# Strassen's products on eight of sixteen blocks of values and gate in six heads, in place of four

## The chip, the cores and the metric

The kernel runs on one core of one Trainium2 chip. The metric is the device time of one execution in microseconds (us). Its engines are TensorE (PE, with its weight loads PEld), VectorE (DVE), ScalarE (ACT), GpSimd (POOL) and SyncE (SP), which here only issues loads. Each engine works through its own instructions in a fixed order and waits where an operand or a buffer is not ready.

## The reference

Two layers on 256 tokens of width 2048, in float32: a retention layer (8 heads, keys of 256, values of 512 per head) and a pooling layer. The change touches the projections of the retention layer alone:

```python
def retention_layer(x, g_norm, w_in, gn, w_out):
    h = rms_norm(x, g_norm)
    p = h @ w_in
    q, k, v, z = jnp.split(p, [...], axis=-1)
    q = rope(q...); k = rope(k...) * (RET_HEAD_QK ** -0.5)
    o = chunkwise_retention(q, k, v)
    ...                                    # group norm of o per head
    o = o.astype(x.dtype) * jax.nn.silu(z)
    return o @ w_out
```

Per head, v and z (the gate) are each `[256, 2048] @ [2048, 512]`.

## The kernel before

**Precision.** Every operand of a float32 product is split into a part `hi` that TensorE takes in its float32r form and a rest `lo`: ScalarE casts `hi` (L98), VectorE subtracts `lo = src - hi` (L99). A product is then three matmuls, hi·hi, hi·lo and lo·hi, added up in one bank of PSUM (`Sum.add`, L195).

**Tiles.** The 2048 inputs of the projection are 16 blocks of 128, the tokens two halves of 128. Weights arrive in units of `[128, 2048]` float32 (1 MB), three of which can be in flight or in use (`raw`, `bufs=3`); their split halves live in five buffers of 1024 columns of hi and of lo (`w`, `bufs=5`).

**A head** takes twelve units: four for queries and keys (QK units: 16 pairs of a 512- and a 256-column matmul each, L129 and L130, into banks 4 to 7, evicted as `hl` and `qk` by L138 and L139), and eight for values and gate, in the order of `HEAD_ORDER`. Between the two lie the rotation of queries and keys on VectorE (`tcos`, `tsin`, `qk`, L338 to L342, then the split into `qs`), the scores (`sc`, ten matmuls, bank 4) and their mask (`sm`, L361 to L363). A unit of kind v or z holds four blocks of values or of gate and costs 24 matmuls of 512 columns. A unit S holds two blocks of each, `strassen_blocks` says which, and `strassen_unit` takes them by Strassen's seven products, 21 matmuls: VectorE first forms sums of weight blocks from the raw unit (`tc`, L221; `ts`, L223 and L224), which are split like weights (`w<-tc`, `w<-ts`); the sums on the side of the activations (`forms`) are made once, in head 0, by `sides` and lie in a part of `os` that the last head fills. The products p1, p5, p6, p7 lie in banks 5, 6, 4 and 7, and c11, c21 (values) and c12, c22 (gate) in banks 0 to 3. After the last S unit L388 to L392 combine the p's; at the end of a head follow `vs`, `po`, the group norm (`ors`), `og`, and eight transposes (`turned`, L453) that are split into `os` (L103, L104) while TensorE is at the next head's QK units.

**Order.** The program is written head by head; a scheduler then lays each engine's instructions in an order of its own, which is fixed when the program is built. VectorE and ScalarE thus prepare units ahead of TensorE, as far as five `w` buffers let them.

Of the kernel before, what the change touches and what calls it, by code (L numbers as in the profile page):

```python
# [13 lines left out]
P = 128  # L14
D = 2048
S = 256
KT = D // P
NH = 8
DV = 512
VT = 2 * D // P  # L20
# [12 lines left out]
SUMS = ("p1", "p5", "p6", "p7", "c11", "c21", "c12", "c22")  # L33


HEAD_ORDER = ("vvvvzzzz",) + ("vvvSzSzz",) * (NH - 1)
HEAD_BANKS = {"c11": 0, "c21": 1, "c12": 2, "c22": 3, "p6": 4, "p1": 5, "p5": 6, "p7": 7}


def strassen_blocks(first, j):  # L40

    k = first + 4 * (j // 2) + j % 2
    return k, k + 2
# [7 lines left out]
def kernel(  # L51
# [56 lines left out]
    def load(src):  # L108
        raw = wpool.tile([P, UNIT], F32, tag="raw", name="raw", bufs=3)
        nc.sync.dma_start(out=raw, in_=src)  # L110
        return raw
# [138 lines left out]
    hs = act.tile([P, KT, 2, S], F32R, tag="hs", name="hs")  # L250


    with tc.tile_pool(name="rt", bufs=1) as rt:
# [10 lines left out]
        for u in range(4):  # L264
# [6 lines left out]
            for i in range(2):  # L271
                w = wpool.tile([P, 2, HALF], F32R, tag="w", name="w", bufs=5)
                hi, lo = w[:, 0], w[:, 1]
# [42 lines left out]
        unit = 4  # L316


        forms = os[:, VT - 4 :].rearrange("p k a s -> p (k a s)").rearrange("p (i f l t) -> p i f l t", f=4, l=2, t=P)

        def tokens(k, t):
            ts = slice(t * P, (t + 1) * P)
            return hs[:, k, 0, ts], hs[:, k, 1, ts]

        for h in range(NH):
# [40 lines left out]


            order = HEAD_ORDER[h]
            strassen, plain = order.count("S"), {"v": 2 * order.count("S"), "z": 2 * order.count("S")}
            sums = {}  # L370
            for name, i in HEAD_BANKS.items():
                n = 3 * strassen * (name != "c22") + 12 * order.count("v") * (name[0] == "c")
                if n:
                    sums[name] = Sum(i, name, n)
            vt = rt.tile([P, 2, DV], F32, tag="vt", name="vt")
            gz = rt.tile([P, 2, DV], F32, tag="gz", name="gz")
            done = 0
            for kind in order:
                unit += 1
                if kind == "S":  # L380
                    s = [rt.tile([P, 2, 512], F32, tag=tag, name=tag[:2]) for tag in ("tcos", "tsin")]
                    k1, k2 = strassen_blocks(0, done)
                    strassen_unit(
                        load(ret_in[unit - 1]), s, (tokens(k1, 0), tokens(k2, 0), tokens(k2, 1)), forms[:, done], sums
                    )
                    done += 1
                    if done == strassen:
                        nc.scalar.copy(vt[:, 0], sums["p1"].tile)  # L388
                        nc.vector.tensor_tensor(out=vt[:, 1], in0=sums["p6"].tile, in1=vt[:, 0], op=ALU.add)
                        nc.vector.tensor_tensor(out=gz[:, 0], in0=sums["p5"].tile, in1=vt[:, 1], op=ALU.subtract)  # L390
                        nc.vector.tensor_tensor(out=vt[:, 1], in0=sums["p7"].tile, in1=vt[:, 1], op=ALU.add)
                        nc.vector.tensor_tensor(out=gz[:, 1], in0=sums["p5"].tile, in1=vt[:, 1], op=ALU.subtract)  # L392
                    continue
                halves = weights(ret_in[unit - 1])
                for i, (hi, lo) in enumerate(halves):
                    for j in range(2):
                        for t in range(2):
                            ws = slice(j * 512, (j + 1) * 512)
                            sums[f"c{t + 1}{1 + 'vz'.index(kind)}"].add(*tokens(plain[kind], t), hi[:, ws], lo[:, ws])
                        plain[kind] += 1  # L400


            vs = rt.tile([P, 2, 2, DV], F32R, tag="vs", name="vs")
# [26 lines left out]
                nc.scalar.activation(sq, po[t], AF.Square, accum_out=var[:, t : t + 1])  # L430
            nc.vector.tensor_scalar(out=var, in0=var, scalar1=1.0 / DV, scalar2=EPS, op0=ALU.mult, op1=ALU.add)
            rsqrt(ors, var)
            if h == 0:
                a = rt.tile([P, 4, S], F32, tag="tcos", name="a")
                x = rt.tile([P, 2, P], F32, tag="tsin", name="x")
                sides(hs, 0, 0, a, x, forms)


            og = rt.tile([P, 2, DV], F32, tag="tcos", name="og")
# [260 lines left out]
def _layout(inputs):  # L700

    import numpy as np

    f = np.float32

    def units(w):
        k, n = w.shape
        w = w.reshape(k // P, P, n // P, P).transpose(2, 1, 0, 3).reshape(n // P, P, k)
        if k == 2 * UNIT:
            w = w.reshape(n // P, P, 2, UNIT).transpose(0, 2, 1, 3)  # L710
        elif 2 * k == UNIT:
            w = w.reshape(n // P // 2, 2, P, k).transpose(0, 2, 1, 3)
        return np.ascontiguousarray(w).reshape(-1, P, UNIT)

    def head_units(v, z, order):
        units, j = [], 0
        plain = {"v": 2 * order.count("S"), "z": 2 * order.count("S")}
        for kind in order:
            if kind == "S":
                k1, k2 = strassen_blocks(0, j)  # L720
                units.append(np.stack([z[k1], v[k1], z[k2], v[k2]]))
                j += 1
            else:
                units.append((v if kind == "v" else z)[plain[kind] : plain[kind] + 4])
                plain[kind] += 4
        return np.stack(units).transpose(0, 2, 1, 3).reshape(-1, P, UNIT)

    def mixed_units(w, first):
        w = w.reshape(VT, P, 4, 512)
        units = []  # L730
        for c in (0, 2):
            classic, j = iter(CLASSIC), 0
            for kind in ORDER:
                if kind == "C":
                    k, i = next(classic)
                    k4 = 4 * classic_blocks(first)[k]
                    units.append(w[k4 : k4 + 4, :, c + i])
                else:
                    k1, k2 = strassen_blocks(first, j)
                    units.append(np.stack([w[k1, :, c + 1], w[k1, :, c], w[k2, :, c + 1], w[k2, :, c]]))  # L740
                    j += 1
        return np.stack(units).transpose(0, 2, 1, 3).reshape(-1, P, UNIT)

    def by_partition(v):
        return v.reshape(-1, P).T

    w = inputs["ret_w_in"][0]
    q = units(w[:, :D]).reshape(NH, 2, P, UNIT)
    k = units(w[:, D : 2 * D]).reshape(NH, 2, P, UNIT)
    v = w[:, 2 * D : 4 * D].reshape(KT, P, NH, DV)  # L750
    z = w[:, 4 * D :].reshape(KT, P, NH, DV)
    vz = np.stack([head_units(v[:, :, h], z[:, :, h], HEAD_ORDER[h]) for h in range(NH)])
    ret_in = np.concatenate([q, k, vz], axis=1).reshape(-1, P, UNIT)
    first = ret_in[:4].reshape(4, P, 4, 4, P).transpose(2, 1, 3, 0, 4).reshape(4, P, UNIT)
    ret_in = np.concatenate([first, ret_in[4:]])
    w = inputs["pool_w_in"][0]
    u = units(w[:, : 2 * D]).reshape(NG, GT, P, UNIT)
    z = units(w[:, 2 * D :]).reshape(NG, GT, P, UNIT)
    pool_in = np.concatenate([u, z], axis=1).reshape(-1, P, UNIT)
    pool_grp = np.concatenate([units(m) for m in inputs["pool_w_grp"][0]])  # L760

    vecs = np.concatenate(
        [
            by_partition(inputs["ret_norm"][0]),
            by_partition(inputs["pool_norm"][0]),
            by_partition(inputs["ret_gn"][0]),
            by_partition(inputs["pool_b_grp"][0]),
            by_partition(inputs["pool_scale"][0]),
        ],
        axis=1,  # L770
    )

    half = np.arange(P, dtype=f)
    inv = f(10000.0) ** (-half / f(P))
    ang = np.arange(S, dtype=f)[None, :] * inv[:, None]
    rope = np.stack([np.cos(ang), np.sin(ang)], axis=1)
    lg = np.log1p(-np.exp2(f(-5.0) - np.arange(NH, dtype=f)))
    diff = (np.arange(S)[None, None, :] - np.arange(S).reshape(2, P, 1)).astype(f)
    m = np.where(diff[None] >= 0, np.exp(np.maximum(diff, f(0.0))[None] * lg[:, None, None, None]), f(0.0))
    masks = (m * f(1.0 / 16.0)).transpose(0, 2, 1, 3).reshape(NH, P, 2 * S)  # L780
    masks = np.concatenate([masks[:, :, :S], masks[:, :, S + P :]], axis=2)
    t = np.arange(S)
    icnt = np.stack([f(1.0) / np.minimum(t + 1, w).astype(f) for w in WINDOWS])
    icnt = np.broadcast_to(icnt[None], (P, NG, S))

    return {
        "xT": inputs["x"][0].T.reshape(KT, P, S).transpose(1, 0, 2),
        "xN": inputs["x"][0].reshape(2, P, D).transpose(1, 0, 2),
        "ret_in": ret_in,
        "ret_out": mixed_units(inputs["ret_w_out"][0], FIRST[0]),  # L790
        "pool_in": pool_in,
        "pool_grp": pool_grp,
        "pool_out": mixed_units(inputs["pool_w_out"][0], FIRST[1]),
        "vecs": vecs,
        "g_last": np.broadcast_to(inputs["final_norm"], (P, D)),
        "rope": rope,
        "masks": masks,
        "icnt": icnt,
        "ident": np.eye(P, dtype=f),
    }  # L800
# [18 lines left out]
```

## Time and profile before

| | |
|---|---|
| median of 3 runs | 1362.15 us (1361.92 to 1362.23) |
| the profiled execution | 1361.73 us |
| its span in the trace | 1359.4 us |
| TensorE busy | 1347.6 us, 99% |
| weight loads / VectorE / ScalarE busy | 84% / 79% / 54% |
| one middle head (239.06 to 307.94 us) | 68.88 us |

The span runs from the first to the last recorded instruction; 2.3 us of the profiled execution lie around it. Busy shares are averages over the span; for this change the stretch of one head matters, which repeats seven times from 101 us on.

### The profile page before, as it was taken

The page shows a single profiled execution, that of the slowest core. Times are in us where ns is not written, and L with a number is a line of the kernel's source. Part 1 is how long each engine was busy: PE and PEld are TensorE (multiplying, and loading weights), DVE is VectorE, ACT ScalarE, POOL GpSimd, SP SyncE. Part 2 cuts the span into 40 slices and gives each one's busy share as a digit, 9 for nine tenths or more (in the row PEclk, how much of TensorE's full clock was granted, in tenths as well). Part 3 has the DMA queues.
Part 4 walks back from the last instruction along what each step waited for, and adds up shares of the span by engine and source line. Part 5 has one row for each costly group of instructions (what it writes and reads, how often), then busy time and mean ns, then how long its engine had stood idle before and what let it go on. Part 6 is the DMA issues. An engine that isn't in the chain of part 4 may idle for free.

```text
span 1359.4 us, 17755 instructions
## 1 busy us (share of the span) xinstructions
PE 1347.6 (99%) x6846; PEld 1145.6 (84%) x6846; DVE 1073.6 (79%) x1550; ACT 731.6 (54%) x1031; POOL 25.5 (2%) x34
## 2 busy tenths in 40 slices
PE   9999999999999999999999999999999999999997
PEld 7888888888888888878888888888888888888886
DVE  7868787878787878798677867876886896888676
ACT  7455555555555555555555545445545545555444
POOL 0000000000000000000000000000000000000102
PEclk9999999999999999999999999999999999999999
DMA  8555546464645455575556555555555555555552
GB/s 338 182 192 174 203 164 213 161 217 161 213 164 200 171 193 177 188 247 201 181 185 213 188 190 187 190 200 190 196 190 186 187 188 192 191 207 212 186 214 95
DMA packets 38196, 262.64 MB, mean 193 GB/s; under 512 B 4368, under 2 KB 4496, under 8 KB 7392
## 3 DMA queue, kind: packets, MB, share of 16 engines
q1 hardware_dynamic: 36432, 255.41, 54.3%
q0 software_dynamic: 1536, 5.57, 1.3%
q8 instruction: 54, 0.88, 0.2%
q10 hardware_dynamic: 144, 0.52, 0.1%
q14 instruction: 30, 0.25, 0.0%
HBM read 259.39 MB, written 2.10 MB: 192 GB/s over the span
## 4 chain that ended last, share of the span: by engine, by line
PE 98%; DVE 1%; ACT 0%; DMA 0%; issue 0%; DVEq 0%; SPq 0%; ACTq 0%
PE c L195 43%; PE acc L129 29%; PE acc L130 15%; PE p L195 6%; PE po L427 1%; PE acc L286 1%; PE acc L287 1%; PE turned L453 1%; PE sc L352 0%; DMA xin<-in_ret_in 0%; PE sc L357 0%; ACT w L98 0%; PE turned L562 0%; DVE w L99 0%; DVE tsin L339 0%; DVE tcos L338 0%
## 5 line engine op out<-in xcount | busy, mean ns | idle before, releaser
L99 DVE TENSOR_TENSOR w<-raw,w 128x1024 fp32r<-128x1024 f32 x472 | 558.1, 1192 | 140.7 <-ACT w L98 136.4
L98 ACT CAST w<-raw 128x1024 fp32r<-128x1024 f32 x472 | 479.1, 1026 | 275.5 <-PE c L195 172.8
L129 PE MATMUL acc<-hs,w 128*128 128x512 f32 x1472 | 516.3, 394 | 0.0
L130 PE MATMUL acc<-hs,w 128*128 128x256 f32 x1472 | 413.4, 281 | 0.0
L129 PEld LDWEIGHTS acc<-hs,w 128*128 128x128 f32 x1472 | 275.7, 187 | 61.8
L195 PE MATMUL c<-w,hs 128*128 128x512 f32 x1284 | 303.9, 390 | 0.0
L195 PEld LDWEIGHTS c<-w,hs 128*128 128x128 f32 x1284 | 239.1, 188 | 49.6
L130 PEld LDWEIGHTS acc<-hs,w 128*128 128x128 f32 x1472 | 278.0, 189 | 1.8
L195 PE MATMUL c<-w,os 128*128 128x512 f32 x666 | 162.6, 392 | 0.0
L195 PE MATMUL c<-w,gs 128*128 128x512 f32 x624 | 147.1, 390 | 0.0
L195 PEld LDWEIGHTS c<-w,os 128*128 128x128 f32 x666 | 124.4, 188 | 26.8 <-ACT w L98 0.3
L195 PEld LDWEIGHTS c<-w,gs 128*128 128x128 f32 x624 | 117.0, 188 | 24.8
L138 ACT COPY hl<-acc 128x256 f32<-128x256 f32 x96 | 35.6, 372 | 147.2 <-PE acc L130 147.2
L129 PE MATMUL acc<-ms,w 128*128 128x512 f32 x256 | 89.0, 390 | 0.0
L130 PE MATMUL acc<-ms,w 128*128 128x256 f32 x256 | 72.2, 282 | 0.0
L98 ACT CAST w<-s 128x1024 fp32r<-128x1024 f32 x32 | 33.5, 1049 | 53.9 <-PE c L195 48.6
L99 DVE TENSOR_TENSOR w<-s,w 128x1024 fp32r<-128x1024 f32 x32 | 39.1, 1223 | 24.6 <-ACT w L98 24.5
L129 PEld LDWEIGHTS acc<-ms,w 128*128 128x128 f32 x256 | 48.0, 188 | 10.1
L130 PEld LDWEIGHTS acc<-ms,w 128*128 128x128 f32 x256 | 48.4, 189 | 0.0
L195 PE MATMUL p<-w,os 128*128 128x512 f32 x150 | 40.9, 390 | 0.0
L195 PE MATMUL p<-w,forms 128*128 128x512 f32 x144 | 39.8, 397 | 0.5 <-ACT forms L98 0.5
L195 PEld LDWEIGHTS p<-w,forms 128*128 128x128 f32 x144 | 27.0, 188 | 7.5 <-ACT forms L98 1.0
(184 smaller groups left out, 1024.7 us busy)
## 6 DMA issues: line engine op xcount, KB each, us to landing
raw<-in_ret_in SPq DMA_DIRECT2D x92, 1024.0 KB, 5.0
raw<-in_pool_in SPq DMA_DIRECT2D x64, 1024.0 KB, 5.0
raw<-in_ret_out SPq DMA_DIRECT2D x32, 1024.0 KB, 5.0
raw<-in_pool_out SPq DMA_DIRECT2D x32, 1024.0 KB, 5.1
raw<-in_pool_grp SPq DMA_DIRECT2D x16, 1024.0 KB, 5.0
xin<-in_ret_in SPq DMA_DIRECT2D x3, 1024.0 KB, 11.4
xn<-in_xN POOLq DMA_DIRECT2D x4, 512.0 KB, 6.8
out<-xn SPq DMA_DIRECT2D x8, 256.0 KB, 2.3
```

What stands on the lines that cost most here:

```text
L98: nc.scalar.copy(hi, src)
L99: nc.vector.tensor_tensor(out=lo, in0=src, in1=hi.bitcast(F32), op=ALU.subtract)
L129: nc.tensor.matmul(acc, hi, moving[:, k], start=(k == 0), stop=False)
L130: nc.tensor.matmul(acc[:, :S], lo, moving[:, k, 0], start=False, stop=(k == n - 1))
L138: nc.scalar.copy(t, acc[:, S:])
L195: nc.tensor.matmul(self.tile, a, w, start=(self.done == 0), stop=(self.done == self.n - 1))
L286: nc.tensor.matmul(accs[c], hi[:, b], hs[:, k], start=(k == 0), stop=False)
L287: nc.tensor.matmul(accs[c][:, :S], lo[:, b], hs[:, k, 0], start=False, stop=(k == KT - 1))
L427: nc.tensor.matmul(po[t], ss[:, p, queries], vs[:, keys, q], start=first, stop=last)
L453: nc.tensor.transpose(turned[:, j * S + t * P : j * S + (t + 1) * P], og[:, t, (2 * i + j) * P : (2 * i + j + 1) * P], idt)
```

## The change

Heads 1 to 6 take four S units in place of two, in the order v S v S S z S z in place of v v v S z S z z. Head 0 (none) and head 7 (two) stay as they were, since the second part of the sums of activations lies where head 6 puts its result. The second pair of sums is made in head 0 by a second call of `sides`. The layout of the weights in memory follows the new order; the bytes stay the same. `head_blocks` gives the order of blocks to kernel and layout alike.

```diff
-HEAD_ORDER = ("vvvvzzzz",) + ("vvvSzSzz",) * (NH - 1)
+HEAD_ORDER = ("vvvvzzzz",) + ("vSvSSzSz",) * (NH - 2) + ("vvvSzSzz",)
+HEAD_FORMS = 4
+def head_blocks(order):
+    products = {k for j in range(order.count("S")) for k in strassen_blocks(0, j)}
+    rest = {c: iter([k for k in range(KT) if k not in products]) for c in "vz"}
+    for kind in order:
+        unit = {"v": "vvvv", "z": "zzzz", "S": ""}[kind]
+        held = [(c, next(rest[c])) for c in unit]
+        yield kind, held
...
-        forms = os[:, VT - 4 :].rearrange(...)
+        forms = [
+            os[:, VT - 4 - 4 * i : VT - 4 * i].rearrange(...)
+            for i in range(HEAD_FORMS // 2)
+        ]
...
-                n = 3 * strassen * (name != "c22") + 12 * order.count("v") * (name[0] == "c")
+                n = 3 * strassen * (name != "c22") + 3 * (KT - 2 * strassen) * (name[0] == "c")
...
-            for kind in order:
+            for kind, held in head_blocks(order):
...
-            if h == 0:
+            for i in range(HEAD_FORMS // 2 if h == 0 else 0):
                 a = rt.tile([P, 4, S], F32, tag="tcos", name="a")
                 x = rt.tile([P, 2, P], F32, tag="tsin", name="x")
-                sides(hs, 0, 0, a, x, forms)
+                sides(hs[:, 4 * i :], 0, 0, a, x, forms[i])
```

The lines of the changed kernel stand lower by 11 to 16: L195 becomes L206, L99 L110, L221 L232, L223 and L224 L234 and L235, L338 to L342 L354 to L358, L352 and L357 L368 and L373, L361 to L363 L377 to L379.

The order of the instructions moves with it. On VectorE, in a middle head, from the rotation's second product to the second subtraction of the head's first S unit, before (`tc` and `ts` are the sums of weight blocks, `qs` the split queries and keys):

```order
L339 TENSOR_TENSOR tsin<-qk,rpr 128x1024
L99 TENSOR_TENSOR w<-raw,w 128x1024
L341 TENSOR_TENSOR qk<-tcos,tsin 128x2x256
L342 TENSOR_TENSOR qk<-tsin,tcos 128x2x256
L99 TENSOR_TENSOR w<-raw,w 128x1024
L221 TENSOR_TENSOR tc<-raw 128x1024
L99 TENSOR_TENSOR w<-raw,w 128x1024
L99 TENSOR_TENSOR qs<-qk,qs 128x4x256
L223 TENSOR_TENSOR ts<-tc,raw 128x512
L99 TENSOR_TENSOR w<-raw,w 128x512
L224 TENSOR_TENSOR ts<-ts,raw 128x512
L99 TENSOR_TENSOR w<-tc,w 128x1024
```

and in the change:

```order
L355 TENSOR_TENSOR tsin<-qk,rpr 128x1024
L115 SCALAR_TENSOR_TENSOR os<-turned,vec,os 128x256
L357 TENSOR_TENSOR qk<-tcos,tsin 128x2x256
L358 TENSOR_TENSOR qk<-tsin,tcos 128x2x256
L232 TENSOR_TENSOR tc<-raw 128x1024
L110 TENSOR_TENSOR qs<-qk,qs 128x4x256
L234 TENSOR_TENSOR ts<-tc,raw 128x512
L110 TENSOR_TENSOR w<-tc,w 128x1024
L235 TENSOR_TENSOR ts<-ts,raw 128x512
L232 TENSOR_TENSOR tc<-raw 128x1024
L377 TENSOR_TENSOR sm<-sc,sm 128x128
L378 TENSOR_TENSOR sm<-sc,mk 128x256
```

The four subtractions on raw weights no longer stand among the rotation (the S unit's own two now stand ahead of it), the last two of the eight `os` pieces of the head before have moved in, and the next S unit's `tc` stands ahead of the mask.

On TensorE, at the same place: ahead of the first S unit stood the 72 matmuls of three v units and all of the scores (rows before, from the last score on):

```order
L357 MATMUL sc<-qs 128x256 x4
L195 MATMUL c_1495<-w,hs 128x512 x3
L195 MATMUL c_1496<-w,hs 128x512 x3
L195 MATMUL p_1500<-w,hs 128x512 x3
L195 MATMUL c_1497<-w,os 128x512 x3
L195 MATMUL c_1495<-w,hs 128x512 x3
L195 MATMUL p_1501<-w,os 128x512 x3
L195 MATMUL p_1502<-w,os 128x512 x3
L195 MATMUL c_1496<-w,hs 128x512 x3
L195 MATMUL p_1499<-w,os 128x512 x3
```

In the change 24 matmuls of one v unit stand there, and then (p_2110 is p1, p_2111 p5, p_2112 p7, p_2109 p6, c_2106 c21):

```order
L206 MATMUL p_2110<-w,hs 128x512 x3
L206 MATMUL c_2107<-w,os 128x512 x3
L206 MATMUL c_2105<-w,hs 128x512 x3
L368 MATMUL sc<-qs 128x256
L206 MATMUL p_2111<-w,os 128x512
L206 MATMUL p_2112<-w,os 128x512
L368 MATMUL sc<-qs 128x256 x5
L373 MATMUL sc<-qs 128x256 x4
L206 MATMUL p_2111<-w,os 128x512 x2
L206 MATMUL p_2112<-w,os 128x512 x2
L206 MATMUL c_2106<-w,hs 128x512
L206 MATMUL p_2109<-w,os 128x512
```

The scores have moved in among the products of the first S unit, and those products are cut into a first matmul (hi·hi) and a later pair (hi·lo, lo·hi).

On VectorE, further on in the change's head, the third and fourth S unit (no such stretch stood before):

```order
L232 TENSOR_TENSOR tc<-raw 128x1024
L110 TENSOR_TENSOR w<-raw,w 128x1024
L110 TENSOR_TENSOR w<-raw,w 128x512
L234 TENSOR_TENSOR ts<-tc,raw 128x512
L110 TENSOR_TENSOR w<-tc,w 128x1024
L235 TENSOR_TENSOR ts<-ts,raw 128x512
L232 TENSOR_TENSOR tc<-raw 128x1024
L110 TENSOR_TENSOR w<-ts,w 128x1024
L110 TENSOR_TENSOR w<-raw,w 128x1024
L234 TENSOR_TENSOR ts<-tc,raw 128x512
L110 TENSOR_TENSOR w<-raw,w 128x1024 x2
L235 TENSOR_TENSOR ts<-ts,raw 128x512
```

The fourth S unit's `tc` now stands ahead of the third's `w<-ts`, and the z unit between them only behind it.

## Rows read from the trace of the kernel before

**Rows 1.** The page, busy time of each engine (share of the span).

```profile
PE 1347.6 (99%) x6846; PEld 1145.6 (84%) x6846; DVE 1073.6 (79%) x1550; ACT 731.6 (54%) x1031; POOL 25.5 (2%) x34
```

**Rows 2.** Waits of TensorE in the whole program: in total, times, longest.

```profile
PE acc L286 <- ACT w L98: 1.9, 1, 1.9
PE cold L257 <- POOL ones_f L247: 1.0, 1, 1.0
PE p L195 <- ACT forms L98: 0.5, 1, 0.5
PE sc L352 <- ACT qs L98: 0.2, 1, 0.2
```

**Rows 3.** Stretches: length; busy PE, PEld, DVE, ACT, POOL; granted clock; DMA share, GB/s.

```profile
239.06:307.94 68.88, 68.88 (x342) 58.20 (x342) 55.48 (x77) 38.03 (x52) 0.54 (x1) 1.00 0.55 186
...
238.80:284.70 45.90, 45.90 (x212) 38.24 (x211) 40.24 (x48) 26.37 (x33) 0.54 (x1) 1.00 0.59 197
284.70:307.70 23.00, 23.00 (x134) 19.98 (x133) 15.24 (x30) 11.66 (x20) 0.00 (x0) 1.00 0.47 165
...
78.10:101.80 23.70, 23.70 (x140) 20.91 (x139) 18.07 (x37) 12.84 (x24) 0.00 (x0) 1.00 0.47 166
```

**Rows 4.** Timeline of TensorE: start, length, line, what.

```profile
59.55 0.38 PE L352 MATMUL sc<-qs 128*128 128x256 f32 x1 [0.17 <-ACT qs L98]
59.79 5.53 PE L195 MATMUL c<-w,hs 128*128 128x512 f32 x23
...
238.89 12.22 PE L195 MATMUL c<-w,hs 128*128 128x512 f32 x53
250.95 0.28 PE L352 MATMUL sc<-qs 128*128 128x256 f32 x1
...
254.05 0.75 PE L352 MATMUL sc<-qs 128*128 128x256 f32 x5
254.64 0.64 PE L357 MATMUL sc<-qs 128*128 128x256 f32 x4
...
301.45 0.82 PE L453 MATMUL turned<-idt,og 128*128 128x128 f32 x6
...
302.22 0.40 PE L129 MATMUL acc<-hs,w 128*128 128x512 f32 x1
```

**Rows 5.** Timeline of VectorE, from the last `qk` of a head on.

```profile
241.16 1.22 DVE L339 TENSOR_TENSOR tsin<-qk,rpr 128x1024 f32<-128x1024 f32 x1
242.29 1.22 DVE L99 TENSOR_TENSOR w<-raw,w 128x1024 fp32r<-128x1024 f32 x1
243.43 0.68 DVE L341 TENSOR_TENSOR qk<-tcos,tsin 128x512 f32<-128x512 f32 x1
244.03 0.69 DVE L342 TENSOR_TENSOR qk<-tsin,tcos 128x512 f32<-128x512 f32 x1
...
250.38 0.69 DVE L224 TENSOR_TENSOR ts<-ts,raw 128x512 f32<-128x512 f32 x1
251.14 1.23 DVE L99 TENSOR_TENSOR w<-tc,w 128x1024 fp32r<-128x1024 f32 x1
252.40 1.23 DVE L221 TENSOR_TENSOR tc<-raw 128x1024 f32<-128x1024 f32 x1
254.01 1.23 DVE L99 TENSOR_TENSOR w<-ts,w 128x1024 fp32r<-128x1024 f32 x1 [0.38 <-ACT w L98]
...
255.88 0.28 DVE L361 TENSOR_TENSOR sm<-sc,sm 128x128 f32<-128x128 f32 x1
256.09 0.41 DVE L362 TENSOR_TENSOR sm<-sc,mk 128x256 f32<-128x256 f32 x1
...
302.48 0.88 DVE L104 SCALAR_TENSOR_TENSOR os<-turned,vec,os 128x256 fp32r<-128x256 f32 x2 [1.45 <-ACT os L103]
303.28 0.41 DVE L139 TENSOR_TENSOR qk<-acc,hl 128x256 f32<-128x256 f32 x1
```

**Rows 6.** Timeline of ScalarE: the cast of `w<-ts` ahead of VectorE's at 254.01.

```profile
252.93 1.05 ACT L98 CAST w<-ts 128x1024 fp32r<-128x1024 f32 x1 [1.82 <-PE c L195]
```

More of the change, by code (lines that the diff above doesn't have):

```diff
@@ L316 @@
         unit = 4
-        forms = os[:, VT - 4 :].rearrange("p k a s -> p (k a s)").rearrange("p (i f l t) -> p i f l t", f=4, l=2, t=P)
+        forms = [
+            os[:, VT - 4 - 4 * i : VT - 4 * i].rearrange("p k a s -> p (k a s)").rearrange(
+                "p (i f l t) -> p i f l t", f=4, l=2, t=P
+            )
+            for i in range(HEAD_FORMS // 2)
+        ]
         def tokens(k, t):
@@ L368 @@
             order = HEAD_ORDER[h]
-            strassen, plain = order.count("S"), {"v": 2 * order.count("S"), "z": 2 * order.count("S")}
+            strassen = order.count("S")
             sums = {}
             for name, i in HEAD_BANKS.items():
-                n = 3 * strassen * (name != "c22") + 12 * order.count("v") * (name[0] == "c")
+                n = 3 * strassen * (name != "c22") + 3 * (KT - 2 * strassen) * (name[0] == "c")
                 if n:
@@ L383 @@
                     strassen_unit(
-                        load(ret_in[unit - 1]), s, (tokens(k1, 0), tokens(k2, 0), tokens(k2, 1)), forms[:, done], sums
+                        load(ret_in[unit - 1]), s, (tokens(k1, 0), tokens(k2, 0), tokens(k2, 1)), forms[done // 2][:, done % 2], sums
                     )
@@ L394 @@
                 halves = weights(ret_in[unit - 1])
[L395 to L400, printed above, removed]
+                for i, (column, k) in enumerate(held):
+                    hi, lo = halves[i // 2]
+                    for t in range(2):
+                        ws = slice(i % 2 * 512, (i % 2 + 1) * 512)
+                        sums[f"c{t + 1}{1 + 'vz'.index(column)}"].add(*tokens(k, t), hi[:, ws], lo[:, ws])
             vs = rt.tile([P, 2, 2, DV], F32R, tag="vs", name="vs")
@@ L716, in head_units @@
         units, j = [], 0
-        plain = {"v": 2 * order.count("S"), "z": 2 * order.count("S")}
-        for kind in order:
+        for kind, held in head_blocks(order):
             if kind == "S":
@@ L723, in head_units @@
             else:
-                units.append((v if kind == "v" else z)[plain[kind] : plain[kind] + 4])
-                plain[kind] += 4
+                units.append(np.stack([(v if c == "v" else z)[k] for c, k in held]))
         return np.stack(units).transpose(0, 2, 1, 3).reshape(-1, P, UNIT)
```

## Prediction

> **What bounds the kernel now.** I read the shares on the page first: TensorE is busy for 99% of the span, VectorE for 79% [rows 1]. Then the waits of TensorE: four in the whole program, 3.6 us together, two at the start, one at head 0's scores and one (`forms`) in the way out; in the heads with S units it never waits [rows 2]. Then one head by stretches: 68.88 us, in all of which TensorE is busy, VectorE for 55.48 [rows 3]. So a matmul left out in a head is worth its whole time, as long as VectorE and ScalarE still hand over their halves in time. The timeline of TensorE gives the prices: the first 53 matmuls of a head run from 238.89 to 250.95, 0.2275 us each, and five 256-column matmuls of the scores take 0.59 us, 0.12 each [rows 4].
>
> The third reading decides. I cut the head where its QK units end. In the 45.9 us of rotation, values and gate VectorE is busy for 40.24 us, 88%, in the 23.0 us of the QK units for 15.24, 66% [rows 3]. The change puts its new VectorE work into the first of these.
>
> **What the change removes.** An S unit has 21 matmuls where a plain one has 24. Two more S units in six heads leave out 2 x 6 x 3 = 36 matmuls, 8.2 us in all or 1.37 us per head.
>
> **What it adds.** VectorE's instructions follow each other at 1.13 to 1.14 us for 1024 columns and 0.60 for 512; one that waits for the instruction right before it starts 0.15 us later still (250.38 to 251.14 is 0.76) [rows 5]. A plain unit is two subtractions, 2.27 us. An S unit is `tc`, two halves of `ts`, subtractions for 1024 and 512 raw columns and for `tc` and `ts`: four times 1.135 and three times 0.605, 6.35 us. That is 4.08 more per unit, 8.2 more per head. The stretch would hold 40.24 + 8.2 = 48.4 us of VectorE work against 45.9 - 1.37 = 44.5 us of matmuls: 3.9 us per head do not fit, unless VectorE enters the stretch further ahead than now.
>
> The Trainium skill ("Perfetto Trace Analysis", Identifying the Most-Contended Engine) says to find the engine with the highest occupancy and improve that one first, and that for VectorE occupancy is a fair measure of how close it is to its limit. By the shares of the page that is TensorE, with a fifth of VectorE free, and the sum would be the 8.2 us and nothing else. The same page (Optimization Strategy) adds that the most contended engine can change between regimes; the trace agrees, with 88% and 66% in the two stretches of a head.
>
> **The first place of waiting: the first S unit.** Its operands pass through a chain that starts with the last QK eviction. The three v units that covered it, 72 matmuls or 16.4 us, become one, 5.5 us. I walk the change's order with t = 0 at the head's first v matmul. That point is where 302.22 stands in the trace, behind an accumulation behind the six transposes; there VectorE evicts the last `qk` at 303.28, t = 1.06 [rows 4, 5]. Starts on VectorE are then: `os` 1.40, `tcos` 1.80, `tsin` 2.94, `os` 4.07, `qk` 4.47 and 5.07, `tc` 5.83 (with the 0.15), `qs` 6.96, `ts` 8.10, `w<-tc` 8.70, `ts` 9.83, the next unit's `tc` 10.44, mask 11.57 and 11.78 (0.21 apart), `w<-ts` 12.11. An end that another engine waits for is 1.22 after the start (0.69 for 512 columns), a ScalarE cast takes 1.05, and a handover 0.03 [rows 5, 6].
>
> TensorE has 24 matmuls of v, nine of p1, c12 and c11, and one score, which end at t = 7.63. Then it waits:
> - for the cast of `tc` (ends 7.05 + 0.03 + 1.05), until 8.16: 0.5 us;
> - after two matmuls and nine scores, at 9.70, for the rest of `w<-tc` (9.92), until 9.95: 0.25;
> - after four matmuls, at 10.86, for the cast of `ts` (10.52 + 1.08), until 11.63: 0.75;
> - after one of c21, at 11.86, for the mask, which frees bank 4 for p6 (12.19), until 12.21: 0.35;
> - at 12.44 for the cast of the next v unit, behind that of `ts` on ScalarE (12.56): 0.15;
> - at 12.82 for the rest of `w<-ts` (13.33): 0.55.
>
> Together 2.6 us. Behind each of these stand all later matmuls of the head, so nothing else covers it.
>
> **The second place: the third S unit.** From `w<-ts` of the first S unit (12.11) to that of the third, VectorE's order holds ten instructions of 1024 columns, six of 512, the last of the mask, `ss` (an estimate of 0.47, between 0.21 for 128 and 0.60 for 512 columns) and two dependent starts: 11.35 + 3.63 + 0.2 + 0.47 + 0.3 = 15.95, so that it starts at 28.06. Its `ts` is ready 1.2 us earlier, the cast of it at about 27.95. TensorE has 105 matmuls and ten scores until it needs that cast, 25.1 us, and its 2.6 of waiting: it stands there at 27.7. It waits 0.3, then about 0.5 for the cast of the z unit behind it, then 0.2 for that unit's rest: 1.0 us. After it, with 24 + 21 matmuls of z and S and 24 more of z against 6.35 and 2.27 us of VectorE work, VectorE gets ahead again.
>
> **What costs nothing, and why.** The end of a head has one z unit (5.5 us) behind the last S unit in place of two. The first QK unit needs bank 4, freed by the first of the combinations; the order puts three subtractions, 3.4 us, ahead of that, so 2 us are to spare; without them the price would be about 0.6 each for two instructions. ScalarE casts 3584 columns for an S unit in place of 2048, some 1.6 us more at 1.05 per 1024, 3.2 per head, and is busy for 38.03 of 68.88 [rows 3]. Loads stay twelve per head at a DMA share of 0.55. The second pair of activation sums in head 0 is one addition of 1024 and seven instructions of 256 columns, some 3.5 us of VectorE; its QK stretch leaves 5.6 of 23.7 us free [rows 3], and if not, it costs 3.5 once.
>
> **Sum.** Six heads, each 3.6 us of waiting less 1.37: 6 x 2.2 = 13.2. The profiled execution took 1361.73, of which the span is 1359.4; 1361.73 + 13.2 = 1374.9. The median of the runs is 0.4 above the profiled one: 1375.
>
> **Bounds.** Waiting has hardly any row in the heads of before. Its price from below: if each of the nine waits is shorter by a dependent start, 0.15, and a little more, 2.0 us per head remain: +3.8, 1366. From above: the 3.9 us that do not fit, and at each of nine waits a slow restart, which the nearest row puts at 0.12 (after the wait at 59.55 the next matmul starts 0.24 later, not 0.12 [rows 4]), 5.0 us per head: +21.8, 1384. I take the walk, since its prices are the head's own.
>
> **Rivals.**
> 1. *The gain arrives.* If VectorE prepares more in the QK stretch, where 7.8 of 23.0 us are free, its deficit of 3.9 vanishes. Then 1362.15 - 8.2 = 1354.0. The point from which this decides is 1.37 us of waiting per head. This is where the skill's rule of the highest occupancy leads. Against it: five `w` buffers hold no more than two and a half units, and the chain from the last `qk` cannot start earlier whatever is prepared. 8%.
> 2. *Waiting and saving cancel.* Waits between 0.9 and 1.8 us per head give a time within 0.2% of before, 2.7 us, which is about what a measurement of this kernel tells from no change: 1362. It would need the second place to fall away and the first to halve. 6%.
> 3. *VectorE falls behind for good.* If in the first stretch half of its 5.7 us of idle time stays as waiting for casts, it takes 40.24 + 8.2 + 2.8 = 51.3 where 45.9 were: +5.4 per head, 1394. For it: the change leaves it handovers in both directions. Against it: ScalarE is free enough to run ahead. 6%.
>
> The forecast as worked out: 80%. The clock gets no term: the granted clock is 1.00 in every stretch [rows 3].
>
> **Numbers.** 1375, range 1366 to 1384, which holds the forecast's own 80% and both bounds. Faster by over 0.2%: 8%; within 0.2%: 6%; slower: 86%.
>
> **What would show it.** In the changed profile a head with four S units takes about 71 us in place of 68.88, and TensorE waits in it at two places, 2.6 us around the scores and 1.0 some 16 us later, put down to casts (`w`, L109) and subtractions (L110); in head 7 there is none. VectorE is busy for nearly all of the first 45 us of such a head. The prediction is wrong if TensorE's waits in a head stay under 1.4 us, or if they lie in the QK units, which I expect to stay free.

## The result, and the profile after

| | before | changed |
|---|---|---|
| median of the runs | 1362.04 us | 1373.99 us (1373.89 to 1374.09) |
| ratio | 1 | 1.0088, 95% interval 1.0074 to 1.0102 |
| span in the trace | 1359.4 us | 1371.8 us |

The changed kernel is 12 us slower; 1375 was forecast. The page's busy times first, which answer to [rows 1]:

```profile
PE 1351.3 (99%) x6810; PEld 1136.8 (83%) x6810; DVE 1120.1 (82%) x1619; ACT 750.4 (55%) x1059; POOL 25.5 (2%) x34
```

The 36 matmuls are gone (6846 to 6810), and yet TensorE is recorded as busy for 3.7 us longer. VectorE has 46.5 us more. Then the waits of TensorE in the whole program (total, times, longest), against [rows 2]:

```profile
PE c L206 <- ACT w L109: 4.5, 12, 0.5
PE acc L297 <- ACT w L109: 2.0, 1, 2.0
PE p L206 <- ACT w L109: 1.9, 6, 0.3
PE p L206 <- DVE w L110: 1.3, 6, 0.2
...
```

The first and the two `p L206` lines are new; each comes once or twice in each of the six heads. Two stretches of one such head, against [rows 3] (columns as there):

```profile
243.10:288.60 45.50, 44.06 (x192) 34.57 (x191) 44.12 (x53) 26.76 (x34) 0.54 (x1) 1.00 0.50 175
288.60:314.06 25.46, 25.46 (x147) 22.14 (x146) 18.56 (x35) 14.10 (x24) 0.00 (x0) 1.00 0.55 191
```

The head has 70.96 us where it had 68.88. In the stretch of rotation, values and gate VectorE works 44.12 of 45.50 us, 97%; in the QK stretch TensorE never stands still. The granted clock stays at 1.00.

The stretches of [rows 3] end 2.35 us inside the QK units, which start at 282.35. Cut at the same place as the two above, the head before is:

```profile
238.80:282.35 43.55, 43.55 (x199) 36.19 (x197) 38.12 (x46) 24.22 (x30) 0.54 (x1) 1.00 0.58 198
282.35:307.70 25.35, 25.35 (x146) 22.03 (x145) 17.36 (x32) 13.81 (x22) 0.00 (x0) 1.00 0.49 166
```

So the first stretch is 1.95 us longer than before and holds 6.0 us more of VectorE work; in the QK stretch 1.2 us were added.

The waits as listed add up to 1.3 us per head, too little for 2.1 us more in spite of 1.37 us of matmuls less. The timeline of TensorE shows why: what counts is the distance from one start to the next.

```profile
243.10 5.64 PE L206 MATMUL c<-w,hs 128*128 128x512 f32 x24
...
250.62 0.28 PE L368 MATMUL sc<-qs 128*128 128x256 f32 x1
251.22 0.73 PE L206 MATMUL p<-w,os 128*128 128x512 f32 x2 [0.33 <-ACT w L109]
251.80 0.76 PE L368 MATMUL sc<-qs 128*128 128x256 f32 x5
252.40 0.63 PE L373 MATMUL sc<-qs 128*128 128x256 f32 x4
253.01 1.19 PE L206 MATMUL p<-w,os 128*128 128x512 f32 x4
254.75 0.49 PE L206 MATMUL c<-w,hs 128*128 128x512 f32 x1 [0.55 <-ACT w L109]
255.38 0.47 PE L206 MATMUL p<-w,os 128*128 128x512 f32 x1
255.70 0.49 PE L206 MATMUL c<-w,hs 128*128 128x512 f32 x1
256.42 0.72 PE L206 MATMUL p<-w,os 128*128 128x512 f32 x2 [0.23 <-DVE w L110]
...
269.99 1.46 PE L206 MATMUL p<-w,os 128*128 128x512 f32 x5
271.28 0.40 PE L206 MATMUL c<-w,hs 128*128 128x512 f32 x1
271.89 0.73 PE L206 MATMUL c<-w,hs 128*128 128x512 f32 x2 [0.21 <-ACT w L109]
272.46 0.62 PE L206 MATMUL p<-w,os 128*128 128x512 f32 x2
```

A score of 0.12 us is followed only 0.60 us after its start, and matmuls of 0.2275 only after 0.63 and 0.72. A wait is recorded only from the end of the matmul before it, and that end is modelled well behind the point where the next could start: of the 0.48 us lost ahead of 251.22, 0.33 are listed as waiting, and of the 0.40 ahead of 255.38 none. From 243.10 to 256.42 TensorE starts 42 matmuls of 512 columns and ten scores, 10.76 us, in 13.32: 2.56 us lost. From there to 272.46 it starts 67 matmuls, 15.24 us, in 16.04: 0.8 lost. Together 3.4 us per head, 6 x (3.4 - 1.37) = 12.2.

### The profile page after: what moved, and what is told of

Same layout as the page of the kernel before. It is cut to its first block, busy times and chain, and to the rows that moved or that the text cites. A ratio compares the mean times of both kernels' runs of the same rounds, so it can differ in the third digit from the quotient of the medians.

```text
span 1371.8 us, 17802 instructions
## 1 busy us (share of the span) xinstructions
PE 1351.3 (99%) x6810; PEld 1136.8 (83%) x6810; DVE 1120.1 (82%) x1619; ACT 750.4 (55%) x1059; POOL 25.5 (2%) x34
## 4 chain that ended last, share of the span: by engine, by line
PE 91%; DVE 6%; ACT 1%; issue 1%; DMA 0%; DVEq 0%; SPq 0%; ACTq 0%
PE c L206 37%; PE acc L140 29%; PE acc L141 15%; PE p L206 7%; PE po L442 1%; PE acc L297 1%; DVE tc L232 1%; DVE os L115 1%; ACT w L109 1%; DVE w L110 1%; DVE tsin L355 1%; DVE tcos L354 1%; PE acc L298 1%; DVE qs L110 0%; DMA xin<-in_ret_in 0%
## 5 line engine op out<-in xcount | busy, mean ns | idle before, releaser
L110 DVE TENSOR_TENSOR w<-raw,w 128x1024 fp32r<-128x1024 f32 x472 | 550.6, 1179 | 115.5 <-ACT w L109 110.5
L109 ACT CAST w<-raw 128x1024 fp32r<-128x1024 f32 x472 | 470.5, 1013 | 234.0 <-PE c L206 129.9
L206 PE MATMUL c<-w,hs 128*128 128x512 f32 x1068 | 265.4, 392 | 4.5 <-ACT w L109 4.5
L206 PEld LDWEIGHTS c<-w,hs 128*128 128x128 f32 x1068 | 198.6, 188 | 52.3 <-ACT w L109 10.7
L206 PE MATMUL c<-w,os 128*128 128x512 f32 x702 | 175.7, 392 | 0.0
L206 PEld LDWEIGHTS c<-w,os 128*128 128x128 f32 x702 | 131.1, 188 | 27.9 <-ACT w L109 0.3
L206 PE MATMUL c<-w,gs 128*128 128x512 f32 x624 | 147.1, 390 | 0.0
L206 PEld LDWEIGHTS c<-w,gs 128*128 128x128 f32 x624 | 117.0, 188 | 24.8
L206 PE MATMUL p<-w,os 128*128 128x512 f32 x258 | 78.8, 402 | 4.0 <-ACT w L109 1.9
L206 PEld LDWEIGHTS p<-w,os 128*128 128x128 f32 x258 | 47.0, 188 | 20.9 <-ACT w L109 5.7
L110 DVE TENSOR_TENSOR w<-s,w 128x1024 fp32r<-128x1024 f32 x32 | 39.1, 1223 | 22.9 <-ACT w L109 22.8
L109 ACT CAST w<-ts 128x1024 fp32r<-128x1024 f32 x26 | 27.3, 1050 | 47.2 <-DVE ts L235 47.2
```

The lines of the kernel that those rows point to most:

```text
L109: nc.scalar.copy(hi, src)
L110: nc.vector.tensor_tensor(out=lo, in0=src, in1=hi.bitcast(F32), op=ALU.subtract)
L206: nc.tensor.matmul(self.tile, a, w, start=(self.done == 0), stop=(self.done == self.n - 1))
```

## Experiments

The theory: TensorE waits at two places, at the first S unit because its operands stand in a chain behind the rotation with one v unit for cover, and behind neighbouring S units. The main rival: VectorE's added work does not fit into a head, wherever it stands. Each ratio is to runs of the kernel before on the same chip, whose medians lie between 1361.98 and 1362.04 us.

### The same work, without the chain: own_buffers

```diff
-s = [rt.tile([P, 2, 512], F32, tag=tag, name=tag[:2]) for tag in ("tcos", "tsin")]
+s = [rt.tile([P, 2, 512], F32, tag=tag, name=tag[:2]) for tag in ("vt", "gz")]
```

and the tiles `vt` and `gz` of a head are made after its last S unit.

> Four S units in six heads as in the change, but the sums tc and ts of an S unit lie in the buffers of vt and gz instead of those of the rotation's two products, so that the first S unit's sums can be formed before the rotation. VectorE's work is the same. Theory (TensorE waits because the first S unit's operands stand in a chain behind the rotation): most of the 2.6 us of waiting at the first S unit goes, about 1.2 us per head remains in all, 1361 us. Rival (VectorE simply has 8.2 us more work per head than fits, wherever it stands): the time stays at 1374.

Measured: 1362.27 us, ratio 1.0003 (0.9994 to 1.0011), 11.7 us less than the change. In VectorE's timeline the sums, now named `vt` and `gz`, are formed ahead of the rotation, and the subtraction on the first (`w<-vt`) stands inside it:

```profile
236.83 0.69 DVE L235 TENSOR_TENSOR gz<-gz,raw 128x512 f32<-128x512 f32 x1
...
240.16 1.23 DVE L354 TENSOR_TENSOR tcos<-qk,rpr 128x1024 f32<-128x1024 f32 x1
241.31 1.22 DVE L355 TENSOR_TENSOR tsin<-qk,rpr 128x1024 f32<-128x1024 f32 x1
242.44 1.22 DVE L110 TENSOR_TENSOR w<-vt,w 128x1024 fp32r<-128x1024 f32 x1
```

One head as a stretch:

```profile
240.16:309.17 69.01, 68.69 (x337) 56.69 (x336) 62.84 (x87) 41.16 (x57) 0.54 (x1) 1.00 0.54 187
```

VectorE is as busy as in the change (62.84 us; 62.68 there), the head 1.9 us shorter. So these 11.7 us are not due to the amount of work; the rival falls. Without waits a head would take 68.88 - 1.37 = 67.5, so 1.5 us are still lost, 1.2 were expected. By TensorE's starts 0.3 us of them lie at the first score, which waits for `qs`, and 1.2 at the third S unit:

```profile
263.17 1.62 PE L206 MATMUL p<-w,os 128*128 128x512 f32 x5
264.63 0.40 PE L206 MATMUL c<-w,hs 128*128 128x512 f32 x1
265.24 0.73 PE L206 MATMUL c<-w,hs 128*128 128x512 f32 x2 [0.21 <-ACT w L109]
```

Six matmuls, 1.37 us, fill the 2.07 from 263.17 to 265.24, and 0.5 more are lost just behind. The second place stays, and grows, when the first is gone.

### The same work, one more v unit ahead: two_v_first

```diff
-HEAD_ORDER = ("vvvvzzzz",) + ("vSvSSzSz",) * (NH - 2) + ("vvvSzSzz",)
+HEAD_ORDER = ("vvvvzzzz",) + ("vvSSzSSz",) * (NH - 2) + ("vvvSzSzz",)
```

> Order v v S S z S S z in the six heads: the same units and buffers, one more v unit (5.5 us of matmuls) ahead of the first S unit. Theory of the chain behind the rotation: the 2.6 us at the first S unit go; two pairs of neighbouring S units leave some 1.7 us of waiting per head behind the second of a pair, so 1362 - 8.2 + 10 = 1364 us. Rival (VectorE's load alone): 1374.

Measured: 1365.81 us, ratio 1.0029 (1.0018 to 1.0040), 8.2 us less than the change. TensorE's timeline in a head: the scores pass without a wait, and the waits stand behind the two neighbouring pairs:

```profile
254.38 0.64 PE L373 MATMUL sc<-qs 128*128 128x256 f32 x4
...
261.08 0.50 PE L206 MATMUL p<-w,os 128*128 128x512 f32 x1 [0.37 <-ACT w L109]
...
262.03 0.73 PE L206 MATMUL c<-w,hs 128*128 128x512 f32 x2 [0.21 <-ACT w L109]
...
277.74 0.74 PE L206 MATMUL c<-w,hs 128*128 128x512 f32 x2 [0.22 <-ACT w L109]
```

A head takes 69.58 us, so 2.1 are lost where 1.7 were expected.

### Fewer S units: three_S

```diff
-    unit = {"v": "vvvv", "z": "zzzz", "S": ""}[kind]
+    unit = {"v": "vvvv", "z": "zzzz", "m": "vvzz", "S": ""}[kind]
-HEAD_ORDER = ("vvvvzzzz",) + ("vSvSSzSz",) * (NH - 2) + ("vvvSzSzz",)
+HEAD_ORDER = ("vvvvzzzz",) + ("vvSmSzSz",) * (NH - 2) + ("vvvSzSzz",)
```

> Three S units in six heads, order v v S m S z S z, where m is a unit of two blocks of values and two of gate. 18 matmuls fewer than before, 4.1 us; VectorE's added work is 4.1 us per head, half of the change's, so that the first stretch of a head holds 44.3 us of VectorE work against 45.2 of matmuls. Theory of the two places: no waiting in either, 1358 us. Rival (every S unit beyond two costs what two more cost in the change, half of +12): 1368.

Measured: 1357.75 us, ratio 0.9971 (0.9960 to 0.9982): faster than both. Two heads that follow each other, as stretches from one rotation to the next:

```profile
239.02:308.94 69.92, 69.92 (x347) 59.01 (x347) 60.64 (x83) 39.15 (x54) 0.54 (x1) 1.00 0.55 193
308.94:375.40 66.46, 66.46 (x333) 56.30 (x332) 57.19 (x82) 39.56 (x56) 0.54 (x1) 1.00 0.53 184
```

The scheduler places the rotation differently in alternate heads, so one looks long and one short; together they are 136.38, 68.19 each, 0.7 under the head before, which is what three matmuls fewer are worth. TensorE is busy throughout, with no wait in these heads. 18 matmuls at 0.2275 are 4.1 us, and 4.3 were gained. This run has one S unit fewer, two v units ahead of the first and no neighbouring S units, all at once: it shows that the saving arrives without the two places, and not what each of the three is worth.

### GpSimd for one of the sums: own_and_pool

In addition to `own_buffers`:

```diff
-        nc.vector.tensor_tensor(out=s[0], in0=b[:, 1:3], ...)
+        (first or nc.vector).tensor_tensor(out=s[0], in0=b[:, 1:3], ...)
...
+    # head units: first = nc.gpsimd if done == 2 and strassen == 4 else None
```

> As with the sums in the buffers of vt and gz, and in the six heads the first sum tc (1024 columns) of the third of four S units is formed by GpSimd instead of VectorE, 1.1 us less for VectorE per head where two S units are neighbours. Theory (both places of waiting gone, TensorE again never waits in a head): 1362 - 6.8 = 1355 us. Rival (GpSimd's sum comes late, at 1.5 us per 512 columns, or slows VectorE by working beside it): 1361 or more, as without GpSimd.

Measured: 1365.92 us, ratio 1.0030 (1.0019 to 1.0042), 3.7 us slower than without GpSimd. The theory's number missed by 11 us and the rival holds. Both engines around the sum, in the timeline:

```profile
257.33 2.40 POOL L232 TENSOR_TENSOR vt<-raw 128x1024 f32<-128x1024 f32 x1 [66.87 <-DVE w L110]
257.69 3.12 DVE L110 TENSOR_TENSOR w<-gz,w 128x1024 fp32r<-128x1024 f32 x1 [0.51 <-ACT w L109]
```

GpSimd takes 2.40 us, and VectorE's subtraction that starts beside it takes 3.12 in place of 1.22: it ends 1.1 us after GpSimd. This is so in five of the six heads; in the first the held instruction is a part of the mask, which took 0.29 in the change:

```profile
118.16 2.39 POOL L232 TENSOR_TENSOR vt<-raw 128x1024 f32<-128x1024 f32 x1 [98.41 <-DVE w L110]
118.53 2.18 DVE L379 TENSOR_TENSOR sm<-sm,mk 128x128 f32<-128x128 f32 x1
```

In every one of the six heads VectorE is relieved of 1.13 us and loses 1.9. In the profiles these heads are 0.6 to 0.8 us longer than in own_buffers, 4.3 together; the medians differ by 3.7.

### More in the chain: rotation_twice and rotation_twice_before

In the change, and in the kernel before, the line of the rotation's first product stands twice:

```diff
 nc.vector.tensor_tensor(out=tcos..., in0=qk, in1=wide(rpr[:, 0], 4), op=ALU.mult)
+nc.vector.tensor_tensor(out=tcos..., in0=qk, in1=wide(rpr[:, 0], 4), op=ALU.mult)
```

> The change with the rotation's first product (tcos, 1.13 us on VectorE) computed twice in every head, the same result written again. Theory of the chain: in the six heads with four S units each us in the chain is a us of waiting, and slightly more at the third S unit behind it, so 1374 + 6.8 to 8 = 1381 to 1382 us. Rival (there is slack in the chain, the waiting comes from elsewhere): 1374 to 1376.

> The kernel before with the rotation's first product computed twice in every head. Theory: three v units cover the chain with about 6 us to spare, so nothing changes: 1362 us. Rival (the kernel before has no slack there either): 1362 + 8 x 1.13 = 1371.

Measured: 1382.42 us (1.0149, 1.0132 to 1.0166) on the change, 8.4 more than without; 1360.57 us (0.9990, 0.9981 to 0.9999) on the kernel before. TensorE's waits in one head of the first, as listed:

```profile
PE p L206 <- ACT w L109: 0.9, 1, 0.9
PE c L206 <- ACT w L109: 0.7, 2, 0.5
PE sc L369 <- ACT qs L109: 0.4, 1, 0.4
PE p L206 <- DVE w L110: 0.2, 1, 0.2
```

Now the first score itself waits for the rotated `qs`. The head takes 72.20 us, 1.3 more for 1.13 us of VectorE work. Under three v units the same work costs nothing. The 0.1% by which the second run was faster was not expected; a head there takes 68.7 us in place of 68.9, and why is open.

### The second pair of activation sums alone: second_forms_only

The kernel before with the loop over `sides(hs[:, 4 * i :], ..., forms[i])` of the change, of which only `forms[0]` is used.

> The kernel before (two S units per head, its order) with the second pair of activation sums made in head 0 as in the change and not used. Theory: hidden, 1362 us. Rival: its 3.5 us of VectorE work lie on the path, 1365.5.

Measured: 1361.67 us, ratio 0.9997 (0.9988 to 1.0007). The page of its profile has VectorE busy for 3.4 us more than before (1077.0 against 1073.6), and they are hidden.

### Fewer buffers: four_w_buffers

```diff
-w = wpool.tile([P, 2, HALF], F32R, tag="w", name="w", bufs=5)
+w = wpool.tile([P, 2, HALF], F32R, tag="w", name="w", bufs=4)
```

> The change with four w buffers in place of five. Rival theory, that the buffers for split weights are too few: the waiting at both places grows, as VectorE can work ahead by a fifth less, by several us per head, 1374 + 6 x 3 = 1392 or more. Theory of the chain and the neighbouring S units: the first place stays at 2.6 us, the other places get somewhat worse, 1379 to 1381, some 2 us of it outside the six heads.

Measured: 1380.40 us, ratio 1.0134 (1.0119 to 1.0149), 6.4 more than the change. A head takes 71.66 us, 0.7 more, 4.3 us in six heads; the other 2 lie outside them. That is the theory's number, and far under the rival's 1392, but the place was missed: the 0.7 us stand at the first place, which was expected to stay at 2.6. TensorE's timeline with two rows of VectorE's, in a head whose first v matmul starts at 245.00:

```profile
246.41 0.69 DVE L110 TENSOR_TENSOR w<-raw,w 128x512 fp32r<-128x512 f32 x1
...
251.39 1.23 DVE L232 TENSOR_TENSOR tc<-raw 128x1024 f32<-128x1024 f32 x1
...
252.52 0.36 PE L368 MATMUL sc<-qs 128*128 128x256 f32 x1
253.83 0.73 PE L206 MATMUL p<-w,os 128*128 128x512 f32 x2 [0.94 <-ACT w L109]
```

A subtraction of 512 raw columns, done ahead of the head in the change, now stands between the last `qk` eviction and the rotation. `tc` starts at t = 6.39 in place of 5.76, and TensorE goes on 1.31 us after the score in place of 0.60. So fewer buffers cost time by lengthening the chain. A sixth buffer was not tried, so that more buffers might help the second place is not excluded.

## Why the prediction was right

**What bounds it.** TensorE in the heads of before, as said: with three S units and no waits the saving arrives in full.

**What is saved.** 8.2 us for 36 matmuls; three_S puts half of them at 4.3.

**What is added.** The term was too large. A head with four S units has 62.68 us of VectorE work, 7.2 more than the 55.48 of [rows 3], where 8.2 were worked out. The count of instructions is right; but in the kernel before 13 subtractions per head waited for a cast, in the change six, and an instruction that follows the one before it without a gap overlaps it by some 0.09 us (1.22 long, 1.13 apart). That is some 0.6 of the 1.0. The wrong cut of [rows 3] changed little: VectorE's shares in the two stretches of before are 88% and 68% with the right one, 88% and 66% as read. Neither carried the sum, which came from the walk.

**The first place.** The walk stands almost to the row. VectorE's starts, with t = 0 at 243.10, in its timeline:

```profile
244.16 0.41 DVE L150 TENSOR_TENSOR qk<-acc,hl 128x256 f32<-128x256 f32 x1
...
248.86 1.23 DVE L232 TENSOR_TENSOR tc<-raw 128x1024 f32<-128x1024 f32 x1
...
251.74 1.22 DVE L110 TENSOR_TENSOR w<-tc,w 128x1024 fp32r<-128x1024 f32 x1
...
254.81 0.42 DVE L378 TENSOR_TENSOR sm<-sc,mk 128x256 f32<-128x256 f32 x1
255.15 1.22 DVE L110 TENSOR_TENSOR w<-ts,w 128x1024 fp32r<-128x1024 f32 x1
```

That is t = 1.06, 5.76, 8.64, 11.71 and 12.05, where 1.06, 5.83, 8.70, 11.78 and 12.11 were worked out. TensorE goes on at t = 8.12, 9.91, 11.65, 12.28, 12.60 and 13.32 (worked out: 8.16, 9.95, 11.63, 12.21, 12.59 and 13.37). Together 2.56 us, forecast 2.6. That the chain through the buffers of the rotation is the cause, and not only where the waits are seen, is shown from three sides: moved out of the chain (own_buffers), covered by one more v unit (two_v_first) and lengthened (rotation_twice; four_w_buffers too, though not planned so).

The prediction also named a sign of being wrong: waits of TensorE under 1.4 us in a head. The waits as listed are 1.3, and by them it would have failed. The prediction did not say how a wait is to be read; the starts, with 3.4 us lost, and the head's 70.96 us where about 71 were forecast bear it out.

**The second place.** It lies where it was put, 15 us after the first (between 269.99 and 272.46), but with 0.15, 0.4 and 0.1 us lost, 0.65 in all, where 0.3, 0.5 and 0.2 were forecast: the term was 0.35 too large. The walk in turn left out that TensorE starts slowly after a wait, by some 0.1 us each time (two matmuls from 251.22 to 251.80 are 0.58 apart, not 0.455), which stood in the upper bound alone. Most of these starts lie under the next wait; one of them, behind the first place, makes up most of the rest of the 0.8. Net, the forecast is 0.2 us per head too large, and with six heads that is the 1 us by which 1375 missed 1374; that it is no more is in part luck. The cause of the second place, neighbouring S units of 6.35 us on VectorE against 4.8 on TensorE, is borne out by two_v_first, where the waits stand behind both pairs, and by own_buffers, where the third S unit still waits, but no run removed this place by itself with four S units.

**What costs nothing.** The QK stretch and the end of a head show no wait of TensorE, nor does head 7; the second activation sums are hidden, as their run shows (they are nine instructions, where eight were counted).

**Rivals.** In these runs the saving arrives only with the chain covered and a smaller dose of S units (three_S); with four of them, neither breaking the chain nor covering it is enough. "The gain arrives" and "waiting and saving cancel" are not what the change does, but the second is what own_buffers does: 1362.3. VectorE does not fall behind for good: the stretch takes 45.50 us, not 51.3, and in the QK units that follow TensorE does not wait. The rule of the Trainium skill by which the engine with the highest occupancy is improved first ("Perfetto Trace Analysis", Identifying the Most-Contended Engine) would have given the saving alone; the sentence on regimes in the same page (Optimization Strategy) is the one that this trace bears out: the weight loads are busy for 76% of the stretch that decides against VectorE's 97%, and for 87% against 73% in the QK stretch.

## What to carry to other kernels

Fewer instructions on the busiest engine pay only as far as its suppliers keep pace in the same stretch: compare the busy times there, and not over the span. They are a first sign and do not decide: with the same VectorE work a head lost 3.4 us or 1.5, by the buffer of the sums alone. Look at what a block moved forward in the order needs first, and how many matmuls stand between that and the chain behind it; here a buffer that two steps share made the chain, and giving the sums another tile took back the 12 us, though not the 8 us that were to be saved. When a saving costs a supplier work, a smaller dose (three S units, 4 us faster) can be better than the full one.

## What was not expected of the hardware

VectorE and GpSimd hold each other up, and the one that starts second pays. In own_and_pool a VectorE subtraction of two float32 tensors of 1024 columns took 3.06 to 3.12 us where a GpSimd addition of 2.40 had started ahead of it, and 1.22 alone. The trace of the kernel before has it both ways, in the pooling layer:

```profile
1246.23 1.29 POOL L671 TENSOR_TENSOR xn<-xn,gb 128x512 f32<-128x512 f32 x1 [59.27 <-ACT sqn L664]
1246.39 2.22 DVE L99 TENSOR_TENSOR w<-raw,w 128x1024 fp32r<-128x1024 f32 x1
...
1256.13 2.35 DVE L99 TENSOR_TENSOR w<-raw,w 128x1024 fp32r<-128x1024 f32 x2
1257.10 2.53 POOL L671 TENSOR_TENSOR xn<-xn,gb 128x512 f32<-128x512 f32 x1 [9.58 <-ACT sqn L664]
```

GpSimd first: it takes 1.29, VectorE 2.22, and ends 1.1 us after GpSimd. VectorE first: its two subtractions take their usual time, GpSimd 2.53, and ends 1.15 us after VectorE. So the price of own_and_pool could have been read before it ran. The Trainium skill ("GPSIMD Engine Reference", Specifications) lists GpSimd's interfaces to on-chip memory as shared with VectorE, with contention for instructions that have two inputs there; the trace agrees, with these numbers.

A wait of TensorE that is listed is shorter than the time lost: 1.3 us per head were listed where 3.4 were lost between starts, and TensorE is recorded as busy for 99% in either kernel.
